# Low parts of streamed weights: a negation on ScalarE and an accumulating DMA in place of a subtraction on VectorE or GpSimd

## The chip, the cores and the metric

The kernel runs on one core of a Trainium2 chip. The metric is the device time of one execution in microseconds (us), the median of several runs.

## What is computed

A bidirectional encoder trunk on 16 meta tokens and 512 real tokens, 1024 features, float32. Four layers stand one after the other: latent attention (MLA), differential attention, a bidirectional recurrent block (RG-LRU), and MLA again. Each is followed by a SwiGLU feed-forward block, and each of these eight sub-layers has an RMS norm before and after it.

```python
for i in range(DEPTH):
    u = _rms_norm(h, g[0])
    u = _mla(u, ...)            # i = 0, 3; _diff_attn for i = 1, _rglru_block for i = 2
    h = h + _rms_norm(u, g[1])
    u = _swiglu(_rms_norm(h, g[2]), ffn_w_in[i], ffn_w_out[i])
    h = h + _rms_norm(u, g[3])
return h[:, N_META:]
```

## The kernel before

Activations lie feature-major in SBUF, 128 features by 528 tokens, so that each projection takes its weights as the stationary operand. A float32 operand x is split into x = h + l: h is x rounded to float32r, l is the rest. A product is three passes, `xh wh`, `xl wh` and `xh wl`, that add up in PSUM (`mm3`, L340 to L346; the matmul is L327). For a block of 128 input features TensorE takes the three in that order, on two ranges of 272 and 256 tokens. So it needs a block's `wl` last, and a `wl` that isn't there stops it at the third pass, since it works in order.

The weights are packed on the host into 456 chunks in the order of their use: mostly 1024 columns (512 KB), else 768, 640 or 512. Class `Weights` streams them. `fetch` loads a chunk with a DMA on SyncE's queue into one of two buffers `ws`. `ensure` makes the parts: ScalarE casts `ws` to `wh` (L261), and the engine named in `l_engine` subtracts, `wl = ws - wh` (L262). There are four pairs of `wh` and `wl`. `next` hands a chunk out and first calls `ensure` for the chunk two later (`ahead=2`), and each `ensure` asks for the load of the chunk two later still.

The order of the work is the order in which the program is written: each engine has one in-order queue, and a manual schedule keeps the written order. So where the calls of `next` and `ensure` stand decides what is ahead of a cast on ScalarE and ahead of a subtraction on its engine.

`run` goes through eight stages, each a sub-layer; `boundary` ends one and starts the next. In a boundary the residual is updated in two halves of the tokens, and the first three output tiles of the next projection are made from four chunks. `l_engine` is GpSimd in the even stages (MLA, differential attention, RG-LRU) and in most of a boundary, and VectorE in the odd stages (feed-forward) and for the last two chunks that a boundary prepares:

```python
self.W.l_engine = nc.vector if s % 2 else nc.gpsimd
```

Further work of GpSimd: the sums of squares `acc` and `acc2` (L321), rotary products, gates and sums of the recurrent block. In MLA the output projection is worked off in groups of four heads: a chunk pair for it is prepared once a group is done (`wo`, three times between the heads of each MLA).

Names used: `ws` loaded chunk, `wh` and `wl` its parts, `xh` and `xl` the parts of the normed input, `ql` the low part of a query tile, `p` a tile of softmax values (scaled at L769), `pa` and `pb` tiles in PSUM, `hh` and `hl` the parts of the hidden tiles of the feed-forward block.

Of the kernel before, what the change touches and what calls it, by code (L numbers as in the profile page):

```python
"""Bidirectional hybrid encoder trunk (MLA, differential attention, RG-LRU, MLA, each with a
SwiGLU mixer) on one core.

Activations are held feature-major, [128 features, token], so that every projection takes its
weights as the stationary operand in the layout they come in.  A float32 operand x is split
exactly into x = h + l, h being x rounded to float32r and l the rest; a product is the three
float32r passes hh + hl + lh, accumulated in float32.
"""
# [42 lines left out]
def spans(t0):  # L51
    """The ranges of tokens that a product takes at a time: 512 columns fill a bank of PSUM."""
    return ((t0, NT),) if t0 else halves(0)


def col0(t0):
    """The column in PSUM of token 0 of an output tile that starts with token t0."""
    return 512 - t0 if t0 else 512 - SPLIT
# [5 lines left out]
# ---------------------------------------------------------------- weight stream layout  # L64
# [4 lines left out]
def weight_plan():  # L69
    """The weight chunks in the order the program consumes them: for each, its blocks as  # L70
    (array, index into it, first row, columns)."""
# [105 lines left out]
# columns of the table of small parameters  # L177
S_NORM = 0                      # layer, which, k
S_MLA = S_NORM + DEPTH * 4 * NK  # j, 5 (q 3, kv 2)
S_SUB = S_MLA + 10  # L180
S_CW = S_SUB + 1                # 4 taps x 12
S_CB = S_CW + 48                # 12
S_BG = S_CB + 12                # direction, gate, 12
S_LL = S_BG + 48                # direction, 12
S_N = S_LL + 24                 # then 4 * 64 for lambda, the same on every partition

# [15 lines left out]
def shape_tables():  # L202
    """Rotary cosines and signed sines in the layout [x1 x2 x1 x2] x token, -|q - k| as a band, and
    for the first 32 queries, repeated."""
# [11 lines left out]
def f32(ap):  # L216
    return ap.bitcast(F32)


class Shifted:  # L220
    """An SBUF tile that is indexed as the output tile in PSUM it was copied from."""
# [8 lines left out]
class Weights:  # L230
    """Streams the weight chunks: DMA in, split into the float32r parts."""
# [8 lines left out]

    def fetch(self, upto):
        while self.n_dma < min(upto + 1, len(self.widths)):
            j = self.n_dma
            n = self.widths[j]
            t = self.k.wpool.tile([P, 1024], F32, name="ws", tag="ws", bufs=2)
            self.k.nc.sync.dma_start(
                out=t[:, 0:n],
                in_=self.dram[self.offs[j]:self.offs[j] + P * n].rearrange("(p n) -> p n", p=P))
            self.stage[j] = t
            self.n_dma += 1  # L250

    def ensure(self, upto):
        upto = min(upto, self.low + self.BUFS - 1, len(self.widths) - 1)
        while self.n_split <= upto:
# [7 lines left out]
            self.l_engine.tensor_tensor(out=wl[:, 0:n], in0=s[:, 0:n], in1=f32(wh[:, 0:n]), op=ALU.subtract)  # L262
# [12 lines left out]
    def retire(self, n):  # L275
        """All products with the first n of the held chunks have been traced."""
        self.low += n


class Trunk:  # L280
# [26 lines left out]
    # ---------------------------------------------------------------- small helpers  # L307
# [32 lines left out]
    def mm3(self, outs, wh, wl, xh, xl, start, stop, louts=None):  # L340
        """outs[i] += (wh + wl)^T (xh[i] + xl[i]) without the l l term; louts are the outputs for the
        xl[i], if those come in other ranges."""
# [5 lines left out]
    def xr(self, k, rng, hrng=None):  # L348
        """The two halves of input tile k: h parts (or those of the ranges hrng) and l parts."""
        hs = [self.xh[:, k, a:b] for a, b in hrng or rng]  # L350
        ls = [self.xl[k, int(a >= SPLIT)][:, a - (SPLIT if a >= SPLIT else 0):b - (SPLIT if a >= SPLIT else 0)]
              for a, b in rng]
        return hs, ls
# [5 lines left out]
    def project(self, t0=0, mid=None, ahead=2):  # L359
        """One output tile of 128 features from the normed input, K = 1024; mid is traced halfway."""  # L360
# [12 lines left out]
    def project_parts(self, done):  # L373
        """The same in four parts to be traced apart; done gets the finished tile."""
# [15 lines left out]
    # ---------------------------------------------------------------- norms  # L390
    def rstd(self, ps, out, inv_n, late=False):
        """out = 1 / sqrt(ps * inv_n + eps): the table's value, then a Newton step (returned to be
        traced later, if late)."""
# [9 lines left out]
    def stat(self, srcs):  # L403
        """Sums over the partitions of the given [128, w] tiles, on every partition."""
# [6 lines left out]
    # ---------------------------------------------------------------- between sub-layers  # L411
# [13 lines left out]
    def evict_u(self, m, view, a, b, g, add):  # L425
        """Keep u * g of output tile m and add its squares."""
# [21 lines left out]
    def residual(self, k, a, b, g2, first, last):  # L448
        """h += (u g) r on a half of tile k, and the next sub-layer's input from it, in three
        steps that are traced apart."""  # L450
# [33 lines left out]
    def load_x(self, k, half):  # L484
        """Two tiles of the input on a half of the tokens."""
# [13 lines left out]
    def boundary(self, tail, g1, g2, t0, first=False, last=False, after=None):  # L499
        """Ends a sub-layer (tail traces its last output tiles, one half of the tokens after the  # L500
        other) and starts the next one: the residual update, the norm, and the first three output
        tiles of the next projection."""
# [6 lines left out]
        def adv(n):  # L509
            """Traces n more steps of the updates, three tiles in flight."""  # L510
# [105 lines left out]
    def lead(self, get_chunks, kt, n, nk, t0=0):  # L616
        """The products of the first n output tiles with the first nk blocks: for each tile, in parts
        of two blocks to be traced apart."""
# [15 lines left out]
    def final(self, get_chunks, kt, g1, t0, split, add=False):  # L634
        """Output projection: all but the last split tiles; returns the tail for those, which traces
        a tile on a range of tokens, with mid called part of the way through and done after each
        chunk of weights that isn't the last."""
# [48 lines left out]
    def paired(self, g):  # L686
        """get_chunks for group g of four blocks of an output projection whose chunks hold two tiles each."""
# [6 lines left out]
    def chunked(self, sizes):  # L694
        """get_chunks for an output projection whose tiles each take chunks of these sizes."""
# [10 lines left out]
    # ---------------------------------------------------------------- SwiGLU  # L706
# [32 lines left out]
    # ---------------------------------------------------------------- multi-head latent attention  # L739
    def rope(self, ps, scale, t0, eng):  # L740
        """cos * x + sin * swap(x) of a [x1 x2 x1 x2] tile, times scale."""
# [13 lines left out]
    def softmax_max(self, p, ps, rows):  # L755
        """Takes a [rows, 528] tile of scaled scores from PSUM, negated, with minus its maximum along
        the free axis."""
# [5 lines left out]
    def softmax_exp(self, p, st, rows):  # L763
        """exp(s - max s) and its sums."""
# [7 lines left out]
    def transpose_p(self, ptiles, qts, kt, c0=C0, fold=None):  # L772
        """Columns kt of the P [q, k] tiles as a tile of P^T [k, q] in PSUM (for tile 0 with the 16
        columns that follow); fold, if given, picks the rows of query tile 0 and adds them."""
# [11 lines left out]
    def put_pt(self, ps, kt, t0):  # L786
        """The float32r parts of a tile of P^T; for tile 0 stacked, h h l."""
# [11 lines left out]
    def meta_values(self, n, width):  # L799
        """n tiles [96, width] for the values of the first 16 keys, stacked h l h, with zeros between."""  # L800
# [9 lines left out]
    def put_meta(self, vm, src):  # L810
        """Fills the rows of such a tile from [16, width] in PSUM."""
# [9 lines left out]
    def pv(self, outs, pt, kt, vm, vh, vl, t0):  # L821
        """Adds key tile kt to O^T = V^T P^T, held as two half tiles."""
# [9 lines left out]
    def mla(self, tiles, i, j, t0):  # L832
# [149 lines left out]
        def attend(h):  # L982
            """Scores and softmax of head h, between the transposes and products with the values
            of head h - 1; yields what is left of the latter."""
# [118 lines left out]
    def ps_like_rope(self, t):  # L1103
        """Rotary embedding of the shared key, from SBUF."""
# [11 lines left out]
    # ---------------------------------------------------------------- differential attention  # L1116
    def diff(self, tiles, i):
# [11 lines left out]
        def place(d, x, h, dtype):  # L1129
            """A tile of head h in one of its two places, which hold first its norm, then its parts."""  # L1130
# [32 lines left out]
        def scaled_q(h, dst, ps):  # L1163
            """q / 8 / slope of head h, the slope being the power of two 2^-(h + 1)."""
# [15 lines left out]
        def put_v(h, ps):  # L1180
            """Values of head h, token-major."""
# [16 lines left out]
        def more():  # L1198
            """Traces the next fillings."""
# [7 lines left out]
        def attend(h):  # L1207
            """Scores and softmaxes of head h, between the transposes and products with the values
            of head h - 1 and what there is to fill in."""
# [4 lines left out]
            def trail(n):  # L1214
                """exp of tile n, the scaling of tile n - 1, the difference of tile n - 2."""
# [22 lines left out]
            def score_meta(st):  # L1238
                """Query tile 0: component 0 in rows 0:16, component 1 in rows 32:48."""
# [72 lines left out]
        def sub_norm(hs):  # L1312
            """Per-head RMS norms of O^T over its 128 features, from their squares."""
# [64 lines left out]
        def first_half(m):  # L1378
            """The products of output tile m with the first four heads, in two parts."""
# [40 lines left out]
    # ---------------------------------------------------------------- RG-LRU  # L1420
    def lru_consts(self):
        """8 softplus(-lambda) and its negative, [128, 24] each (direction, tile)."""
# [250 lines left out]
```

## Time and profile before

| | |
|---|---|
| runs | 3310.26, 3317.22, 3307.76 us; median 3310.26 |
| profiled execution | span 3308.6 us from its first to its last instruction; its time outside the span isn't listed apart from the runs |
| mean granted TensorE clock | 0.978 |
| TensorE matmul, weight load | 3128.2 us (95%), 2905.0 us (88%) |
| VectorE, ScalarE, GpSimd | 1880.8 us (57%), 1394.0 us (42%), 751.8 us (23%) |
| read from HBM | 225.34 MB, 69 GB/s over the span |

The profile is of one execution. Busy time of an engine is the union of its instructions. PE is TensorE's matmul, PEld its weight load, DVE is VectorE, ACT is ScalarE, POOL is GpSimd, SP is SyncE; a q behind a name is the engine's queue. An L with a number is a line of the kernel. In lines that group instructions the form is out<-in with buffer numbers left out.

### The profile page before, as it was taken

The numbers are of one execution on the slowest core, as the hardware profiler recorded it, in microseconds if no ns is written. First come the engines' busy times: TensorE is split into PE (matmuls) and PEld (weight loads), VectorE is DVE, ScalarE is ACT, GpSimd is POOL, SyncE is SP. The second block draws the span as 40 slices with busy tenths as digits, with TensorE's granted clock in tenths as the row PEclk, the third lists the DMA queues.
The fourth block names the chain that finished last, engine by engine and source line by source line (L and its number), as shares of the span: only waits on it lengthen the run. The fifth ranks groups of instructions, "written<-read, shape, count | busy, mean of one in ns | idle before, by whom it ended". The sixth has DMA issues, their size and how long they took to land. (4 is left out here: it accounts for less than half of the span.)

```text
span 3308.6 us, 53371 instructions
## 1 busy us (share of the span) xinstructions
PE 3128.2 (95%) x22368; PEld 2905.0 (88%) x22368; DVE 1880.8 (57%) x2993; ACT 1394.0 (42%) x2464; POOL 751.8 (23%) x514
## 2 busy tenths in 40 slices
PE   8999999999989998999988889999998999999998
PEld 7888888999978888999977889999987787788887
DVE  7766667443186767444278874544257666674433
ACT  5544445222255665222245554322235554452222
POOL 3223123000144534000045543000033322330001
PEclk9999999999999999999998999999999999999999
DMA  3111012222211111322321112222321111122232
GB/s 100 31 44 43 27 48 72 90 90 92 89 65 46 39 45 57 98 90 88 97 72 58 64 58 90 90 90 88 95 77 39 46 30 47 58 72 93 95 100 79
DMA packets 71600, 230.88 MB, mean 70 GB/s; under 512 B 7824, under 2 KB 12304, under 8 KB 71360
## 3 DMA queue, kind: packets, MB, share of 16 engines
q1 hardware_dynamic: 70144, 225.54, 21.5%
q8 instruction: 176, 2.88, 0.4%
q10 hardware_dynamic: 1216, 1.93, 0.2%
q14 instruction: 64, 0.52, 0.1%
HBM read 225.34 MB, written 2.10 MB: 69 GB/s over the span
## 5 line engine op out<-in xcount | busy, mean ns | idle before, releaser
L327 PE MATMUL pa<-xh,wh 128*128 128x272 f32 (+2 forms) x4120 | 956.6, 304 | 17.4 <-ACT xh L318 7.6
L327 PE MATMUL pa<-xh,wl 128*128 128x272 f32 (+2 forms) x3776 | 892.3, 299 | 3.5 <-POOL wl L262 3.5
L327 PE MATMUL pa<-xl,wh 128*128 128x272 f32 (+1 forms) x3776 | 808.2, 287 | 43.9 <-DVE xl L324 42.9
L327 PEld LDWEIGHTS pa<-xl,wh 128*128 128x128 f32 x3776 | 619.3, 190 | 91.6 <-DVE xl L324 59.8
L327 PEld LDWEIGHTS pa<-xh,wh 128*128 128x128 f32 x4120 | 663.9, 190 | 36.2 <-DVE ql L324 9.1
L327 PEld LDWEIGHTS pa<-xh,wl 128*128 128x128 f32 x3776 | 614.4, 190 | 8.7 <-POOL wl L262 4.0
L262 DVE TENSOR_TENSOR wl<-ws,wh 128x1024 fp32r<-128x1024 f32 (+1 forms) x280 | 330.5, 1183 | 509.8 <-ACT wh L261 509.8
L262 POOL TENSOR_TENSOR wl<-ws,wh 128x1024 fp32r<-128x1024 f32 (+3 forms) x176 | 387.7, 2208 | 763.7 <-ACT wh L261 619.8
L321 POOL TENSOR_TENSOR acc<-acc,t 128x256 f32<-128x256 f32 (+3 forms) x158 | 165.2, 1045 | 1528.3 <-ACT t L318 1524.1
L261 ACT CAST wh<-ws 128x1024 fp32r<-128x1024 f32 (+3 forms) x456 | 440.4, 980 | 156.8 <-DMA ws<-in_w 142.0
L321 DVE TENSOR_TENSOR t<-pa,r 128x528 f32<-128x528 f32 (+1 forms) x193 | 135.5, 703 | 282.1 <-PE pa L327 282.1
L327 PE MATMUL pa<-hh,wl 128*128 128x272 f32 (+2 forms) x1078 | 249.2, 301 | 0.0
L327 PE MATMUL pa<-hl,wh 128*128 128x272 f32 (+2 forms) x1078 | 247.9, 300 | 0.0
L327 PE MATMUL pa<-hh,wh 128*128 128x272 f32 (+2 forms) x1078 | 247.1, 299 | 0.0
L793 ACT CAST pth<-pa 128x528 fp32r<-128x528 f32 (+3 forms) x200 | 118.7, 593 | 269.7 <-PE pa L782 268.3
L337 ACT CAST hh<-t 128x528 fp32r<-128x528 f32 (+1 forms) x88 | 55.5, 630 | 400.9 <-DVE t L321 400.9
L318 ACT ACTIVATE t<-t 128x528 f32<-128x528 f32 (+3 forms) x121 | 72.2, 597 | 294.8 <-DVE t L321 294.2
L327 PEld LDWEIGHTS pa<-hh,wl 128*128 128x128 f32 x1078 | 171.1, 188 | 6.8
L327 PEld LDWEIGHTS pa<-hh,wh 128*128 128x128 f32 x1078 | 171.3, 189 | 5.9
L327 PEld LDWEIGHTS pa<-hl,wh 128*128 128x128 f32 x1078 | 169.4, 188 | 6.8
L321 DVE TENSOR_TENSOR ptl<-pa,pth 128x528 fp32r<-128x528 f32 (+1 forms) x160 | 111.8, 699 | 79.6 <-ACT pth L793 75.3
L782 PE MATMUL pa<-ident,p 128*128 128x128 f32 (+3 forms) x840 | 140.4, 282 | 2.7 <-DVE p L769 2.6
(285 smaller groups left out, 5244.2 us busy)
## 6 DMA issues: line engine op xcount, KB each, us to landing
ws<-in_w SPq DMA_DIRECT2D x344, 512.0 KB, 3.4
ws<-in_w SPq DMA_DIRECT2D x80, 384.0 KB, 3.4
ws<-in_w SPq DMA_DIRECT2D x16, 320.0 KB, 2.9
ws<-in_w SPq DMA_DIRECT2D x16, 256.0 KB, 2.7
out<-h SPq DMA_DIRECT2D x16, 128.0 KB, 1.7
h<-in_x SPq DMA_DIRECT2D x4, 272.0 KB, 3.7
h<-in_x SPq DMA_DIRECT2D x4, 256.0 KB, 4.0
cos<-in_tab ACTq DMA_DIRECT2D x2, 264.0 KB, 4.1
```

What stands on the lines that cost most here:

```text
L261: self.k.nc.scalar.copy(out=wh[:, 0:n], in_=s[:, 0:n])
L262: self.l_engine.tensor_tensor(out=wl[:, 0:n], in0=s[:, 0:n], in1=f32(wh[:, 0:n]), op=ALU.subtract)
L318: return self.nc.scalar.activation(out=out, in_=in_, func=func, **kw)
L321: return (eng or self.nc.vector).tensor_tensor(out=out, in0=a, in1=b, op=op)
L327: self.nc.tensor.matmul(out, lhsT=lhsT, rhs=rhs, start=start, stop=stop)
L337: self.nc.scalar.copy(out=oh, in_=src)
L782: self.nc.tensor.transpose(ps[0:kb - ka, c0 + qa:c0 + qb], ptiles[qt][0:qb - qa, ka:kb], self.ident[0:qb - qa, 0:qb - qa])
L793: self.nc.scalar.copy(out=hi[0:n, w], in_=src)
```

## The change

In `ensure` the subtraction goes. ScalarE writes -`wh` into the `wl` buffer (an activation, `Copy` with scale -1.0), and a DMA that GpSimd issues reads the chunk from HBM a second time and adds it there (`accum_op=ALU.add`), so that `wl` = -`wh` + chunk. The chunk's place in HBM is a method of its own now. `l_engine` is still set but no longer used. Comments are gone, and the lines below `fetch` stand three lower.

```diff
+    def chunk(self, j):
+        n = self.widths[j]
+        return self.dram[self.offs[j]:self.offs[j] + P * n].rearrange("(p n) -> p n", p=P)
+
     def fetch(self, upto):
...
-            self.k.nc.sync.dma_start(
-                out=t[:, 0:n],
-                in_=self.dram[self.offs[j]:self.offs[j] + P * n].rearrange("(p n) -> p n", p=P))
+            self.k.nc.sync.dma_start(out=t[:, 0:n], in_=self.chunk(j))
...
             self.k.nc.scalar.copy(out=wh[:, 0:n], in_=s[:, 0:n])
-            self.l_engine.tensor_tensor(out=wl[:, 0:n], in0=s[:, 0:n], in1=f32(wh[:, 0:n]), op=ALU.subtract)
+            self.k.act(wl[:, 0:n], f32(wh[:, 0:n]), AF.Copy, scale=-1.0)
+            self.k.nc.gpsimd.dma_start(out=wl[:, 0:n], in_=self.chunk(j), accum_op=ALU.add)
             self.parts[j] = (wh, wl)
```

Two places show what this does to the queues. The first is the entry of the first feed-forward stage on VectorE, before the change (`r` is the norm's factor, `t<-pa` the first work on the stage's tiles):

```order
L324 SCALAR_TENSOR_TENSOR r_75<-t_6132,r_75 128x272
L262 TENSOR_TENSOR wl_6137<-ws_5820,wh_6136 128x1024
L324 SCALAR_TENSOR_TENSOR t_6184<-pb_6180,r_75 128x256
L324 SCALAR_TENSOR_TENSOR t_6184<-t_6184,r_75 128x256
L324 SCALAR_TENSOR_TENSOR r_75<-t_6184,r_75 128x256
L262 TENSOR_TENSOR wl_6190<-ws_5882,wh_6189 128x1024
L321 TENSOR_TENSOR t_6199<-t_6178,r_75 128x528
L321 TENSOR_TENSOR t_6202<-pa_5912,r_75 128x528
```

and the same chunks after it, on GpSimd (L324 is now what L321 was, L265 is the accumulating DMA):

```order
L324 TENSOR_TENSOR acc2_73<-acc2_73,t_6160 128x256
L324 TENSOR_TENSOR acc2_73<-acc2_73,t_6169 128x256
L324 TENSOR_TENSOR acc2_73<-acc2_73,t_6176 128x256
L265 DMA wl_6188<-in_w 128x1024
L265 DMA wl_6242<-in_w 128x1024
L265 DMA wl_6266<-in_w 128x1024
```

The two low parts that stood on VectorE between the pieces of the norm are now DMAs on GpSimd's queue, behind the additions of squares of the boundary, of which the last three are shown.

The second place is ScalarE at the same entry, after the change (L263 is the cast, L321 an activation; `hh` is a part of a hidden tile):

```order
L263 CAST wh_6187<-ws_5870 128x1024
L321 ACTIVATE wl_6188<-wh_6187 128x1024
L610 COPY t_6230<-pa_5962 128x528
L321 ACTIVATE r_75<-pb_6232,eps_78 128x256
L321 ACT_TABLE_LOAD
L321 ACTIVATE junk_79<-eps_78 128x1
L263 CAST wh_6241<-ws_5933 128x1024
L321 ACTIVATE wl_6242<-wh_6241 128x1024
L321 ACTIVATE t_6252<-t_6252 128x528
L340 CAST hh0_6258<-t_6255 128x528
```

Behind each cast, and ahead of what followed it, stands the negation of the same chunk.

## Rows read from the trace of the kernel before

**Rows 1.** The page: busy time, share of the span and instructions of each engine.

```profile
PE 3128.2 (95%) x22368; PEld 2905.0 (88%) x22368; DVE 1880.8 (57%) x2993; ACT 1394.0 (42%) x2464; POOL 751.8 (23%) x514
```

**Rows 2.** Stretches: us; busy PE, PEld, DVE, ACT, POOL; granted clock, DMA share, GB/s.

```profile
30.00:502.00 472.00, 449.87 (x3284) 403.09 (x3283) 314.29 (x661) 228.27 (x469) 121.76 (x68) 0.96 0.14 42
549.00:904.00 355.00, 355.00 (x2910) 355.00 (x2909) 138.35 (x154) 100.45 (x134) 8.30 (x7) 1.00 0.29 92
947.00:1264.00 317.00, 299.45 (x2108) 268.01 (x2108) 212.87 (x440) 189.51 (x367) 135.47 (x102) 0.97 0.15 49
...
1709.00:1972.00 263.00, 216.40 (x1580) 211.20 (x1578) 219.30 (x196) 149.94 (x206) 137.08 (x67) 0.91 0.21 66
...
2477.00:2898.00 421.00, 396.50 (x2261) 329.46 (x2260) 281.10 (x555) 212.38 (x420) 119.92 (x68) 0.98 0.15 46
```

**Rows 3.** Waits: who waited for whom, us in total, times, longest us.

```profile
PE pa L327 <- DVE xl L324: 42.9, 55, 2.4
PE pa L327 <- DVE ql L324: 29.4, 16, 2.4
```

**Rows 4.** Timeline near 198 us: start us, us, engine, line, operation, form, idle before.

```profile
197.61 1.98 ACT L261 CAST wh<-ws 128x1024 fp32r<-128x1024 f32 x2
198.09 0.50 DVE L769 TENSOR_SCALAR p<-p,st 128x528 f32<-128x528 f32 x1
198.70 2.71 DVE L769 TENSOR_SCALAR p<-p,st 128x528 f32<-128x528 f32 x1
198.71 4.96 POOL L262 TENSOR_TENSOR wl<-ws,wh 128x1024 fp32r<-128x1024 f32 x2 [8.24 <-ACT wh L261]
201.44 2.79 DVE L321 TENSOR_TENSOR qsa<-t,qsa 64x528 fp32r<-64x528 f32 x1
202.02 0.40 PE L327 MATMUL pa<-xh,wl 128*128 128x272 f32 x2
```

**Rows 5.** Groups of L261 and L262 by shape: busy us, mean ns | idle before.

```profile
L261 ACT CAST wh<-ws 128x1024 fp32r<-128x1024 f32 x344 | 357.4, 1042 | 132.8 <-DMA ws<-in_w 125.1 <-PE pa L327 7.6
L261 ACT CAST wh<-ws 128x768 fp32r<-128x768 f32 x80 | 65.8, 835 | 12.0 <-PE pb L327 6.0 <-DMA ws<-in_w 4.9 <-PE pa L327 0.8
L262 DVE TENSOR_TENSOR wl<-ws,wh 128x1024 fp32r<-128x1024 f32 x236 | 289.1, 1225 | 262.0 <-ACT wh L261 262.0
L262 POOL TENSOR_TENSOR wl<-ws,wh 128x1024 fp32r<-128x1024 f32 x108 | 272.3, 2526 | 343.2 <-ACT wh L261 284.5 <-issue 46.1 <-DVE rpost L324 8.7
```

**Rows 6.** DMA: the loads' queue (packets, MB, share), and all 456 loads' time to landing.

```profile
q1 hardware_dynamic: 70144, 225.54, 21.5%
...
DMA to landing us min/median/max: 2.5/3.4/5.4
```

**Rows 7.** Timeline inside the first feed-forward stage.

```profile
579.86 1.05 ACT L261 CAST wh<-ws 128x1024 fp32r<-128x1024 f32 x1
589.85 0.41 PE L327 MATMUL pa<-xh,wl 128*128 128x272 f32 x2
595.72 0.41 PE L327 MATMUL pa<-xh,wl 128*128 128x272 f32 x2
```

**Rows 8.** Timeline at the entry of the first feed-forward stage.

```profile
545.62 1.04 ACT L261 CAST wh<-ws 128x1024 fp32r<-128x1024 f32 x1
548.80 0.41 PE L327 MATMUL pa<-xh,wl 128*128 128x272 f32 x2
```

**Rows 9.** Timeline at the end of the first feed-forward stage.

```profile
903.67 3.65 POOL L262 TENSOR_TENSOR wl<-ws,wh 128x768 fp32r<-128x768 f32 x2
907.51 0.29 PE L327 MATMUL pb<-hh,wl 128*128 128x272 f32 x1
```

**Rows 10.** Recurrent stage: two lines of the timeline, and the stretch behind them.

```profile
1961.25 2.82 POOL L262 TENSOR_TENSOR wl<-ws,wh 128x1024 fp32r<-128x1024 f32 x1
1964.12 0.51 PE L327 MATMUL pa<-xh,wl 128*128 128x272 f32 x2 [2.87 <-POOL wl L262]
...
1965.40:1968.80 3.40, 3.40 (x18) 3.40 (x17) 3.40 (x6) 3.17 (x6) 0.00 (x0) 0.50 0.27 104
```

## The prediction

> **What bounds the kernel now.** I read the page's busy times first: TensorE is busy for 95% of the span [rows 1]. So a faster VectorE is worth only what TensorE now idles, and a late operand costs in full. The table by stage says where it idles [rows 2]: in the feed-forward stage of 549 to 904 us TensorE is busy for 355.00 of 355.00 us, in the first latent attention (MLA) for 449.87 of 472, in the differential attention for 299.45 of 317, in the recurrent stage for only 216.40 of 263. The granted clock is 1.00 in the first and 0.96, 0.97 and 0.91 in the others. There is nothing to win in the four feed-forward stages, and 111 us of idle time in the four others (the second MLA has 24.5).
>
> The waits of TensorE say who ends it: `ql` and `xl` of VectorE above all [rows 3]. The timeline around 198 us says why [rows 4]: a softmax scaling that takes 0.50 us takes 2.71 us when GpSimd's subtraction starts beside it, and the next product, which reads two tiles, is as slow. So the removed work on GpSimd holds VectorE up, and TensorE waits for the end of that.
>
> **What is removed.** 280 subtractions on VectorE (236 of them 1225 ns) and 176 on GpSimd (108 of 2526 ns) [rows 5]. In the feed-forward stages that is work under a full TensorE: worth nothing. In the others I credit: of the 29.4 us for `ql` 70%, 21 us (most of those waits follow a pair of GpSimd subtractions); of the 42.9 us for `xl` 20%, 9 us, since much of it comes in the second half of a boundary, where GpSimd only adds squares; of the recurrent stage's idle 46.6 us 55%, 26 us (VectorE is busy for 219 of its 263 us, so what is taken off VectorE there counts); of the differential stage's 17.6 us 40%, 7 us. Idle time there also lowers the clock: 0.04 of 472, 0.09 of 263 and 0.03 of 317 us are 52 us of lost clock [rows 2]; I credit 40%, 21 us. Together **84 us**. None of it is credited in full, as GpSimd still issues 456 DMAs, and what those do to VectorE no row shows. Bounds: nothing, and some 140 us.
>
> **What is added.** ScalarE negates every chunk: its nearest row is the cast of the same tile, 1042 ns [rows 5], so 456 of these are about 440 us of an engine that is busy for 42%. They stand right behind the casts. I put their delay of other ScalarE work at 5 us, since the boundary's `xh` come behind them.
>
> What decides is the path from a cast to the product with `wl`. It was a cast and a subtraction; now it is a cast, a negation, and a DMA that starts only after the negation. No row shows an accumulating DMA or one issued by GpSimd. The nearest is the load of the same chunk from SyncE: median 3.4 us from issue to landing, 2.5 to 5.4; its packets take 21.5% of the span for 225.54 MB, so 1.65 us of all sixteen queues for 0.52 MB [rows 6]. An accumulation must read its destination too: I add one more pass, 1.65 us. The Trainium skill ("Collectives: The Full Stack", section "The bandwidth ceiling") says the same of adds inside a DMA: it blames their half rate on two source reads, not on the add; by it the second pass is also 1.65 us, and no run here shows it yet. GpSimd's issue I put, as an estimate, at 1.2 us, halfway between nothing and its pass over such a chunk [rows 5]. So the DMA takes 3.4 + 1.65 + 1.2 = 6.25 us, and with the negation **7.3 us** from the cast's end to a usable `wl` (6.7 us for 768 columns). Lower bound: 1.04 + 3.4 = 4.4 us. Upper: 1.04 + 2 x 5.4, near 12 us.
>
> Against this stands each chunk's margin, from the cast's end to the first product with `wl`:
> - Steady feed-forward: cast ends at 580.91, product at 589.85, margin 8.94 us, the next chunk 5.87 us later [rows 7]. It holds. The queues hold too: 1.65 + 3.3 = 4.95 us for each 5.87.
> - Stage entries: the cast ends at 546.66, the product starts at 548.80: margin 2.1 us [rows 8]. Four feed-forward entries and three others are like this: 7 x 5.2 = 36 us. GpSimd's queue has the last of twelve additions ahead of that DMA there, but it is done by the negation's end.
> - Attention output chunks: cast over by 198.71, product at 202.02, margin 3.4 [rows 4]; three in each MLA: 6 x 3.9 = 23 us.
> - Ends of the feed-forward stages (768 columns): cast over by 903.67, product at 907.51, margin 3.8 [rows 9]: 4 x 2.9 = 12 us.
> - Recurrent stage, where GpSimd's order and not the cast starts the low part: 1961.25, product 1964.12 [rows 10]; 6.25 - 2.9 = 3.4, twice: 7 us.
> - Eight more (start, first MLA chunks, output of the recurrent stage) at 3.3, a little under the others' mean: 27 us.
>
> That is 105 us at 27 places. The chunks behind a feed-forward entry have small margins as well, but their casts hang on VectorE's and ScalarE's chain, from which 1.2 us subtractions go: 2 us each, 8 us. And a stall costs clock: after the 2.87 us at 1964 the granted clock is 0.50 (1.2 GHz) for 3.4 us [rows 10], so 1.7 us lost; I take that for half of 27 places, 23 us. ScalarE's 5 us included, the loss is **141 us**.
>
> **Sum.** 141 - 84 = +57 us on the profiled span of 3308.6; the runs' median stands 1.7 us above that span. So 3367 us.
>
> **Rivals.**
> 1. *The low part is too late everywhere.* From 8.9 us on, each pair of chunks in a feed-forward stage waits as well. At 10 us it is 1.06 us for each of some 84 pairs, 89 us, and 27 x 2.7 = 73 us more at the tight places: 3530 us, and the queues would be close to full (if an accumulation takes over 4.2 us of all sixteen, they bound the stage). For it: loads and accumulations start at about the same moment, since the load's buffer is now free at the cast's end, and the longest landing is 5.4 us [rows 6]. Against it: the loads use 29% of the queues there [rows 2]. Chance 0.2.
> 2. *The relief wins; faster.* One us of latency is worth about 27 us. Below 5.2 us the sum turns. With a DMA as quick as a plain load (latency 4.4 us) the places cost 33 us, clock and ScalarE 10, and the relief is 84: 3270 us. For it: [rows 4], where the two subtractions visibly cost VectorE over 4 us, and 111 us of idle time. Against it: the second read and GpSimd's issue. Chance 0.2.
> 3. *GpSimd's issue holds VectorE up as its subtraction did.* Then only a third of the relief comes: 57 us more, but 6 less at the attention chunks, where a later TensorE hides it: 3420 us. For it: the exclusion in [rows 4]; against it: an issue is shorter than 2.5 us. The Trainium skill ("SBUF — State Buffer", section "Who interferes with whom") has a rule against this change: VectorE in its two-port modes and GpSimd lock each other out, and a GpSimd-issued DMA waits for its descriptors. The 2.71 us scaling agrees as to the lock; of descriptors no row here tells. Chance 0.2.
>
> That the change does not do what it says is excluded by the instruction order: no subtraction is left, and 456 negations and 456 DMAs stand there.
>
> **Numbers.** Forecast 0.4, rivals 0.2 each. The forecast's own spread is some 40 us either way (a latency of 6 to 8.5 us, relief of 60 to 110). A measurement here tells 0.3%, 10 us, from no change. Faster: rival 2 and a little of the forecast, 0.21. Same: 0.08. Slower: 0.71. The range of 3285 to 3545 takes in most of rivals 1 and 2 and all of 3.
>
> **What would show it.** Right: TensorE's waits for `wl` move to DMAs, 3 to 5 us each at entries and attention output chunks; `ql` waits shrink, the scaling takes 0.5 us again; feed-forward interiors keep 355 of 355; DMA share there rises from 0.29 to some 0.8; the accumulating DMA lands in about 6 us. Wrong: landings over 8 us with waits inside the feed-forward stages (rival 1), landings under 4.5 us (rival 2), or slow VectorE pieces beside each issue (rival 3).

## The result and the profile after

The changed kernel takes 3393.9 us (median of 4 runs, 3389.5 to 3396.0), the kernel before on the same chip 3313.7 us. The ratio is 1.0242, with a 95% interval of 1.0220 to 1.0264: slower by 2.4%. The profiled execution has a span of 3387.8 us, 79.2 us more than before. First the page: busy times and two groups (lines that stood below 262 are now three higher, so that L330 is the matmul and L321 the activation), the DMA queues (packets, MB, share), and four of the DMA issues (count, KB each, us to landing).

```profile
PE 3153.4 (93%) x22368; PEld 2927.6 (86%) x22368; DVE 1401.5 (41%) x2713; ACT 1838.3 (54%) x2920; POOL 750.6 (22%) x794
...
L265 POOL DMA_DIRECT2D wl<-in_w x456 | 395.2, 868 | 2054.4 <-ACT wl L321 1836.8
...
L321 ACT ACTIVATE wl<-wh 128x1024 fp32r<-128x1024 f32 (+3 forms) x456 | 454.3, 996 | 14.5
```

```profile
q0 software_dynamic: 65664, 221.28, 38.8%
q1 hardware_dynamic: 70144, 225.54, 20.2%
...
ws<-in_w SPq DMA_DIRECT2D x344, 512.0 KB, 3.5
wl<-in_w POOLq DMA_DIRECT2D x344, 512.0 KB, 6.3
...
ws<-in_w SPq DMA_DIRECT2D x16, 256.0 KB, 2.7
wl<-in_w POOLq DMA_DIRECT2D x16, 256.0 KB, 4.8
```

Beside [rows 1], VectorE has lost 479 us of work and ScalarE has got 444. TensorE, the bound, is busy for 25.2 us more with the same 22368 matmuls, and its idle time went from 180.4 to 234.4 us: 54.0 us. The two make up the 79.2. The accumulating DMA lands in 6.3 us, counted from the start of its issue (as all landings here are), and its queue takes almost twice the time of the plain loads' queue for about the same bytes (221.28 and 225.54 MB). Who ends TensorE's idle time now, against [rows 3]:

```profile
PE pa L330 <- DMA wl<-in_w: 110.7, 38, 6.8
PE pa L330 <- DVE xl L327: 28.7, 48, 1.7
PE pb L330 <- DMA wl<-in_w: 21.8, 5, 6.0
PE pa L330 <- ACT pth L796: 13.8, 8, 1.8
...
PE pa L330 <- DVE ql L327: 4.2, 2, 2.1
```

The old waits have shrunk (`ql` from 29.4 to 4.2 us, `xl` from 42.9 to 28.7). In their place stand 43 waits for the new DMA, 132.5 us, and one that was not there, for ScalarE's `pth` (the rounded part of the transposed softmax values, which ScalarE casts out of PSUM). The same stages as in [rows 2], moved to where they now lie:

```profile
43.00:520.00 477.00, 446.69 (x3281) 401.88 (x3280) 274.22 (x651) 262.03 (x506) 71.78 (x68) 0.96 0.35 77
573.00:929.00 356.00, 355.18 (x2906) 354.97 (x2905) 59.41 (x85) 160.80 (x191) 61.58 (x68) 1.00 0.80 179
982.00:1306.00 324.00, 309.35 (x2156) 277.56 (x2157) 197.12 (x433) 220.66 (x402) 95.97 (x106) 0.96 0.41 93
1764.00:1982.00 218.00, 202.30 (x1578) 199.61 (x1577) 166.96 (x188) 178.59 (x236) 78.12 (x68) 0.97 0.69 152
```

The feed-forward stage is all but untouched (355.18 us busy of 356.00), though the DMA share went from 0.29 to 0.80. The recurrent stage does its 1578 matmuls in 218 us (263 before). So there is a large gain in one place and a larger loss elsewhere. One place of the loss is the entry of the first feed-forward stage, in the timeline (start us, us, engine, line):

```profile
563.46 1.03 ACT L263 CAST wh<-ws 128x1024 fp32r<-128x1024 f32 x1
...
564.53 1.06 ACT L321 ACTIVATE wl<-wh 128x1024 fp32r<-128x1024 f32 x1
...
565.89 0.88 POOL L265 DMA_DIRECT2D wl<-in_w  x1 [1.60 <-PE pb L330]
...
571.39 0.81 PE L330 MATMUL pa<-xh,wl 128*128 128x272 f32 x2 [4.50 <-DMA wl<-in_w]
```

The cast ends at 564.49. In [rows 8] the product came 2.1 us after that, here it comes 6.9 us after: 1.1 for the negation, 0.3 until GpSimd issues, 5.5 for the DMA. TensorE stands still for 4.50 us. The windows of that stall and of what follows it:

```profile
566.80:571.40 4.60, 0.10 (x2) 0.02 (x1) 3.07 (x6) 4.04 (x6) 0.73 (x1) 0.93 0.91 185
571.40:575.00 3.60, 3.60 (x19) 3.60 (x20) 1.57 (x3) 1.93 (x3) 0.13 (x1) 0.61 0.92 203
575.00:580.00 5.00, 5.00 (x43) 5.00 (x43) 1.42 (x2) 1.50 (x3) 0.87 (x1) 1.00 0.65 162
```

After the stall the granted clock is 0.61 on average over 3.6 us, so partly at its lower level (1.2 GHz): 1.4 us more, which stand in the busy column, not in the idle time. TensorE does 19 matmuls there in 3.6 us, and 43 in the next 5.0.

At the first attention output chunk, [rows 4] before, the stall is longer:

```profile
203.14 1.06 ACT L321 ACTIVATE wl<-wh 128x1024 fp32r<-128x1024 f32 x1
204.50 0.87 POOL L265 DMA_DIRECT2D wl<-in_w  x1 [9.54 <-ACT wl L321]
...
206.52 0.87 POOL L265 DMA_DIRECT2D wl<-in_w  x1 [1.15 <-ACT wl L321]
...
212.31 0.81 PE L330 MATMUL pa<-xh,wl 128*128 128x272 f32 x2 [5.66 <-DMA wl<-in_w]
```

From issue to product are 7.8 us here, against 5.5 at the entry: two chunks are prepared together, and while TensorE waits (206.65 to 212.30) the DMA share is 0.97.

### The profile page after: what moved, and what is told of

The parts are those of the page before. It is cut to its first block, busy times and chain, and to the rows that moved or that the text cites. A ratio compares the mean times of both kernels' runs of the same rounds, so it can differ in the third digit from the quotient of the medians.

```text
span 3387.8 us, 54134 instructions
## 1 busy us (share of the span) xinstructions
PE 3153.4 (93%) x22368; PEld 2927.6 (86%) x22368; DVE 1401.5 (41%) x2713; ACT 1838.3 (54%) x2920; POOL 750.6 (22%) x794
## 3 DMA queue, kind: packets, MB, share of 16 engines
q0 software_dynamic: 65664, 221.28, 38.8%
q1 hardware_dynamic: 70144, 225.54, 20.2%
## 5 line engine op out<-in xcount | busy, mean ns | idle before, releaser
L330 PE MATMUL pa<-xh,wl 128*128 128x272 f32 (+2 forms) x3776 | 908.7, 304 | 90.9 <-DMA wl<-in_w 90.9
L330 PE MATMUL pa<-xh,wh 128*128 128x272 f32 (+2 forms) x4120 | 970.4, 308 | 12.4 <-ACT xh L321 9.8
L265 POOL DMA_DIRECT2D wl<-in_w x456 | 395.2, 868 | 2054.4 <-ACT wl L321 1836.8
L330 PE MATMUL pa<-xl,wh 128*128 128x272 f32 (+1 forms) x3776 | 813.3, 289 | 29.5 <-DVE xl L327 28.7
L330 PEld LDWEIGHTS pa<-xh,wl 128*128 128x128 f32 x3776 | 625.1, 193 | 102.7 <-DMA wl<-in_w 97.3
L330 PEld LDWEIGHTS pa<-xh,wh 128*128 128x128 f32 x4120 | 677.9, 193 | 31.6 <-ACT xh L321 10.9
L330 PEld LDWEIGHTS pa<-xl,wh 128*128 128x128 f32 x3776 | 625.6, 191 | 75.6 <-DVE xl L327 43.1
L263 ACT CAST wh<-ws 128x1024 fp32r<-128x1024 f32 (+3 forms) x456 | 445.2, 976 | 76.5 <-PE pa L330 48.1
L321 ACT ACTIVATE wl<-wh 128x1024 fp32r<-128x1024 f32 (+3 forms) x456 | 454.3, 996 | 14.5
L324 DVE TENSOR_TENSOR t<-pa,r 128x528 f32<-128x528 f32 (+1 forms) x193 | 135.5, 703 | 667.5 <-PE pa L330 667.5
L330 PE MATMUL pa<-hh,wl 128*128 128x272 f32 (+2 forms) x1078 | 249.5, 301 | 5.4 <-DMA wl<-in_w 5.4
L330 PE MATMUL pa<-hl,wh 128*128 128x272 f32 (+2 forms) x1078 | 248.1, 300 | 0.0
L324 DVE TENSOR_TENSOR acc<-acc,t 128x272 f32<-128x272 f32 (+2 forms) x18 | 8.3, 463 | 578.5 <-ACT t L321 574.9
L330 PE MATMUL pa<-hh,wh 128*128 128x272 f32 (+2 forms) x1078 | 247.1, 299 | 0.0
L324 POOL TENSOR_TENSOR acc<-acc,t 128x256 f32<-128x256 f32 (+3 forms) x158 | 164.9, 1044 | 324.1 <-ACT t L321 321.4
L321 ACT ACTIVATE t<-t 128x528 f32<-128x528 f32 (+3 forms) x121 | 72.0, 595 | 205.6 <-DVE t L324 205.6
L330 PEld LDWEIGHTS pa<-hh,wl 128*128 128x128 f32 x1078 | 171.1, 189 | 13.4 <-DMA wl<-in_w 6.9
L330 PEld LDWEIGHTS pa<-hh,wh 128*128 128x128 f32 x1078 | 171.2, 189 | 6.0
L330 PEld LDWEIGHTS pa<-hl,wh 128*128 128x128 f32 x1078 | 169.3, 188 | 6.7
L321 ACT ACTIVATE t<-pa 128x528 f32<-128x528 f32 (+2 forms) x46 | 27.7, 602 | 252.3 <-PE pa L330 252.3
```

Source lines behind the costliest of these rows:

```text
L263: self.k.nc.scalar.copy(out=wh[:, 0:n], in_=s[:, 0:n])
L265: self.k.nc.gpsimd.dma_start(out=wl[:, 0:n], in_=self.chunk(j), accum_op=ALU.add)
L321: return self.nc.scalar.activation(out=out, in_=in_, func=func, **kw)
L324: return (eng or self.nc.vector).tensor_tensor(out=out, in0=a, in1=b, op=op)
L330: self.nc.tensor.matmul(out, lhsT=lhsT, rhs=rhs, start=start, stop=stop)
```

## The experiments

My theory: two separate things happen. Taking the subtractions away gains some 80 us, mostly in the even stages; the longer path from a cast to a usable low part costs more, at places where TensorE's margin is shorter than that path, and nothing elsewhere. The rivals: ScalarE's load costs the time, GpSimd's issues hold VectorE up as its subtractions did, or the relief is small.

**The addition left out.**

```diff
             self.k.act(wl[:, 0:n], f32(wh[:, 0:n]), AF.Copy, scale=-1.0)
-            self.k.nc.gpsimd.dma_start(out=wl[:, 0:n], in_=self.chunk(j), accum_op=ALU.add)
```

> The accumulating DMA is left out, so the low parts hold only the negated high parts and the added chunk is missing from the output; the negation on ScalarE stays. Theory (the change gains by taking the subtractions away and loses by low parts that land late): the 132.5 us of TensorE's waits for the DMAs into wl vanish, and the clock that they cost; by the prediction's terms 3308.6 - 84 + 5, so 3230 us, and between 3215 and 3250. Rival (ScalarE's 456 negations cost far more than 5 us, the waits for pth and xh with them): over 3275 us, with these waits still there. Rival (the relief is small): 3300 us or more with no wait for wl.

Measured: 3220.3 us, ratio 0.9726 (0.9696 to 0.9757); span 3214.6. Its page and the first of TensorE's waits:

```profile
PE 3102.0 (96%) x22368; PEld 2882.0 (90%) x22368; DVE 1382.9 (43%) x2713; ACT 1835.5 (57%) x2920; POOL 357.6 (11%) x338
```

```profile
PE pa L329 <- DVE xl L326: 28.7, 43, 1.7
PE pa L329 <- ACT pth L795: 13.8, 8, 1.8
PE pa L329 <- ACT xh L320: 10.1, 5, 5.9
```

This separates the two halves of the change. Relief with ScalarE's cost: 3308.6 - 3214.6 = 94.0 us. What the DMA costs: 3387.8 - 3214.6 = 173.2 us, of which 51.4 are busy time of TensorE (3153.4 - 3102.0; the mean clock is 0.987 here and 0.969 with the DMA) and 121.8 idle time (132.5 of waits for `wl`, less 10.7 of other waits that these stalls hide). ScalarE's load is not the loss: it is all here. It does cost something, the 13.8 us for `pth`. And the issues hold VectorE little: with 456 of them it is busy for 18.6 us more, 41 ns for each, and 7.5 of these us lie in a few taps of the recurrent stage (see the last section).

**A plain DMA in the place of the accumulating one.**

```diff
-            self.k.nc.gpsimd.dma_start(out=wl[:, 0:n], in_=self.chunk(j), accum_op=ALU.add)
+            self.k.nc.gpsimd.dma_start(out=wl[:, 0:n], in_=self.chunk(j))
```

> GpSimd issues a plain DMA into wl in place of the accumulating one, so the low parts hold the chunk itself and the subtraction of the high part is left out of the output; order, issue, HBM traffic and the wait for the negation stay. Theory (the accumulation's own second pass takes 1.65 us of the 6.3 us): landing about 4.7 us, the 43 stalls shorter by 1.6 us each and some clock back, 3300 to 3325 us, queue share of these DMAs near 20%. Rival (the landing time is the issue by GpSimd and the two transfers side by side): landing stays near 6.3 us, 3390 us. If the landing were that of SyncE's loads, 3.5 us, about 3265 us.

Measured: 3332.3 us, ratio 1.0051 (1.0034 to 1.0068). Its queue, issues, landing and the two waits for `wl`:

```profile
q0 software_dynamic: 65664, 221.28, 22.6%
...
L265 POOL DMA_DIRECT2D wl<-in_w x456 | 246.2, 540 | 2137.4 <-ACT wl L321 1943.7
...
wl<-in_w POOLq DMA_DIRECT2D x344, 512.0 KB, 4.7
```

```profile
PE pa L330 <- DMA wl<-in_w: 71.2, 25, 5.5
...
PE pb L330 <- DMA wl<-in_w: 14.1, 5, 4.0
```

The landing is what the theory says, 1.6 us shorter. The time is 7 us above my range: 61 us gained against the changed kernel, since the shorter transfer leaves 85.3 us of the 132.5. The accumulation costs 0.388 x 3387.8 / (0.226 x 3336.2) = 1.74 times the queues' time of a plain DMA, and 0.33 us more of GpSimd for each issue (868 against 540 ns). So one us of latency is worth 61 / 1.6, some 38 us; I had said 27. (One expectation below writes 37.) The two profiled executions, which differ by 51.6 us, would make it 32.

**All subtractions on VectorE**, in the kernel before.

```diff
-            self.l_engine.tensor_tensor(out=wl[:, 0:n], in0=s[:, 0:n], in1=f32(wh[:, 0:n]), op=ALU.subtract)
+            self.k.nc.vector.tensor_tensor(out=wl[:, 0:n], in0=s[:, 0:n], in1=f32(wh[:, 0:n]), op=ALU.subtract)
```

> The kernel before, with all 456 subtractions on VectorE: no DMA, no negation, and GpSimd has no subtraction. Theory A (what holds VectorE up is GpSimd's subtraction beside it): the scaling of p takes 0.5 us throughout, the waits for ql of 29.4 us fall to under 8, the recurrent stage's 263 us shorten by 20 or more; 3255 to 3290 us although VectorE gets 176 subtractions of 1.2 us more. Theory B (it is the amount of VectorE's own work that counts): VectorE, busy for 219 of 263 us there, becomes the bound of the recurrent stage; 3310 us or slower.

Measured: 3266.5 us, ratio 0.9846 (0.9829 to 0.9863). The scaling, whose longest was 2.71 us before, and the recurrent stretch between the first products with `wl` of chunks 223 and 255 (261.00 us before):

```profile
L769 DVE TENSOR_SCALAR p<-p,st x144: 481/496/889, 74.3 to 2831.7; 128x528 f32<-128x528 f32 x128, 16x528 f32<-16x528 f32 x16
```

```profile
1705.90:1936.80 230.90, 202.79 (x1538) 198.47 (x1536) 205.42 (x223) 148.37 (x205) 63.58 (x36) 0.94 0.22 72
```

Theory A holds, with `ql` waits of 7.9 us: VectorE gets 176 subtractions more, and is busy for only 17.3 us more in the whole kernel (1898.1 against 1880.8), while in the recurrent stretch it is busy for 13 us less (205.42, before 218.39). The removed work on GpSimd had been lengthening VectorE's own instructions. No DMA is needed for this half of the relief (3308.6 - 3263.9 = 44.7 of the 94.0 us).

**By place**: VectorE subtracts, except inside the even stages.

```diff
+    ADDED = {*range(5, 48), *range(121, 150), *range(223, 255), *range(345, 388)} - {18, 28, 38, 358, 368, 378}
...
-            self.k.act(wl[:, 0:n], f32(wh[:, 0:n]), AF.Copy, scale=-1.0)
-            self.k.nc.gpsimd.dma_start(out=wl[:, 0:n], in_=self.chunk(j), accum_op=ALU.add)
+            if j in self.ADDED:
+                self.k.act(wl[:, 0:n], f32(wh[:, 0:n]), AF.Copy, scale=-1.0)
+                self.k.nc.gpsimd.dma_start(out=wl[:, 0:n], in_=self.chunk(j), accum_op=ALU.add)
+            else:
+                self.k.nc.vector.tensor_tensor(out=wl[:, 0:n], in0=s[:, 0:n], in1=f32(wh[:, 0:n]), op=ALU.subtract)
```

> The negation and the accumulating DMA only inside the even stages, without the first attention-output chunk of each group (chunks 5 to 47, 121 to 149, 223 to 254 and 345 to 387 but for six); everywhere else VectorE subtracts. Theory (gain and loss lie at different places): almost all waits for wl go, the relief in the even stages stays; 3225 to 3265 us, faster than before by 1.5% or more. Rival (the relief needs VectorE free at the boundaries and in the feed-forward stages too, or DMAs in the even stages slow others): 3290 us or more. If theory A of the run with all subtractions on VectorE holds and VectorE's work costs nothing, the two runs come out alike within 10 us.

Measured: 3278.7 us, ratio 0.9885 (0.9867 to 0.9904). Faster than before, but outside my range, and 12 us behind the run with VectorE everywhere. Its waits say why:

```profile
PE pa L334 <- DMA wl<-in_w: 29.4, 18, 5.7
PE pa L334 <- ACT pth L800: 13.8, 8, 1.8
```

In the recurrent stretch it gains (214.1 us against 230.9), in both MLAs it loses (556.4 against 539.8 up to chunk 52, 518.0 against 508.7 from 338 to 392): there the subtraction on VectorE cost less than what now takes its place. The wait for `pth` (none in the run with VectorE everywhere) comes with the negations, the first chunks of the two MLAs wait for their DMAs (3.54 and 3.97 us), and one more place, chunk 223 ahead of the recurrent stretch, waits for 5.70 us.

**Halves.**

```diff
-            self.k.act(wl[:, 0:n], f32(wh[:, 0:n]), AF.Copy, scale=-1.0)
-            self.k.nc.gpsimd.dma_start(out=wl[:, 0:n], in_=self.chunk(j), accum_op=ALU.add)
+            for a, b in ((0, n // 2), (n // 2, n)):
+                self.k.act(wl[:, a:b], f32(wh[:, a:b]), AF.Copy, scale=-1.0)
+                self.k.nc.gpsimd.dma_start(out=wl[:, a:b], in_=self.chunk(j)[:, a:b], accum_op=ALU.add)
```

> The changed kernel with each negation and each accumulating DMA in two halves of the columns, so the first half can start after half a negation and is a smaller transfer (256 KB, 4.8 us in the changed kernel). The first half is usable about 2 us sooner (0.5 of negation, 1.5 of transfer). Theory (the loss is latency against margin at some 43 places): by the plain-DMA run, where 1.65 us less were worth 61 us, about 74 us less than the changed kernel's 3394, so 3310 to 3330 us, with the waits for wl near 60 us. Rival (912 issues on GpSimd and the fixed part of a DMA eat it): second halves come late, waits for wl stay above 110 us, 3380 us or more.

Measured: 3353.5 us, ratio 1.0109 (1.0086 to 1.0132). A gain of about 40 us where I expected 64 to 84; the time lies between my range and the rival's. The issues and the landing:

```profile
L266 POOL DMA_DIRECT2D wl<-in_w x912 | 811.3, 1064 | 1675.3 <-ACT wl L322 1519.6
...
wl<-in_w POOLq DMA_DIRECT2D x688, 256.0 KB, 6.3
```

A half lands in 6.3 us, not in 4.8: the first of the two in 5.9, the second in 6.7 (medians). An issue's record is 1.06 us long on average, but the two of a chunk overlap: GpSimd is busy for 811.3 us with 912 of them, 0.89 each. So only the half negation and part of the transfer are won; the waits for `wl` fall to 88.9 us. That the halves are late because they share the queues with each other is my reading. A half also moves in pieces of half the length, and no run separates the two.

**The negation first.**

```diff
-            self.k.nc.scalar.copy(out=wh[:, 0:n], in_=s[:, 0:n])
-            self.k.act(wl[:, 0:n], f32(wh[:, 0:n]), AF.Copy, scale=-1.0)
+            self.k.act(wl[:, 0:n], s[:, 0:n], AF.Copy, scale=-1.0)
+            self.k.nc.scalar.copy(out=wh[:, 0:n], in_=s[:, 0:n])
```

> The changed kernel with ScalarE's two instructions of a chunk exchanged: the negation is made from the loaded chunk and stands ahead of the cast, so that the DMA starts one cast (1.04 us) sooner and the high part comes one negation later. Same instructions, same DMAs. Theory: waits for wl shorter by about 1 us at each of 43 places, 37 us less by the plain-DMA run's 37 us for each us of latency: 3345 to 3365 us. Rival (the high part then comes too late at the same places, or what counts is ScalarE's load and not the order): 3385 us or more, with new waits for wh.

Measured: 3349.2 us, ratio 1.0104 (1.0084 to 1.0124), 45 us below the changed kernel; the waits for `wl` are 96.9 us, 35.6 less. The same instructions in another order give back more than half of the loss. Both landings became longer (3.5 and 6.3 us in the changed kernel). That fits with where the next load now starts: 0.7 us after the accumulation's issue, where it started 1.4 us ahead of it (medians).

```profile
ws<-in_w SPq DMA_DIRECT2D x344, 512.0 KB, 6.3
wl<-in_w POOLq DMA_DIRECT2D x344, 512.0 KB, 6.9
```

**VectorE inside all stages**, GpSimd still in the boundaries and at the ends of stages.

```diff
-            self.W.l_engine = nc.vector if s % 2 else nc.gpsimd
+            self.W.l_engine = nc.vector
```

> The kernel before, where only the line in the loop over the stages sets l_engine to VectorE throughout; GpSimd keeps its subtractions in the boundaries and at the ends of stages. Theory (GpSimd's subtraction costs by holding VectorE up inside the even stages; at a boundary VectorE is itself the chain, so a subtraction is better off on GpSimd there): faster than all on VectorE by what the stretch around the first MLA's end lost there (7.6 us of 99.4) and the second's (4.9), so 3245 to 3262 us. Rival (holding VectorE up costs as much in the boundaries): 3268 us or more.

Measured: 3254.1 us, ratio 0.9806 (0.9792 to 0.9821). One line of the kernel before gives 1.9%. The stretch of chunks 38 to 48, the end of the first MLA, takes 96.9 us here and 107.0 with VectorE everywhere: in a boundary GpSimd's subtraction is the better one. That VectorE is itself the chain there is the theory that forecast it; no run shows the chain by itself.

**Mixed**: the same, with the accumulating DMA for 22 chunks inside the recurrent stage (the edit in `ensure` as in the run by place, with `l_engine` in the second branch).

```diff
+    ADDED = {*range(225, 254)} - {233, 235, 240, 244, 245, 249, 250}
...
-            self.W.l_engine = nc.vector if s % 2 else nc.gpsimd
+            self.W.l_engine = nc.vector
```

> As the run with VectorE inside all stages, but 22 chunks inside the recurrent stage (225 to 253 without 233, 235, 240, 244, 245, 249 and 250) by negation and accumulating DMA. Theory (the accumulating DMA pays only where VectorE is the bound and the margin is over 8 us): the recurrent stretch, 261 us before and 230.9 with all on VectorE, takes 212 to 220 us, so 11 to 18 us less than that run: 3230 to 3248 us, faster than both kernels by over 2%. Rival (VectorE is not the bound there once GpSimd's subtraction is gone): no gain over that run.

Measured: 3237.8 us, ratio 0.9764 (0.9747 to 0.9781), the fastest kernel of the study that does the whole computation: 4.7% below the changed kernel (0.9764 / 1.0242). The recurrent stretch without and with these DMAs:

```profile
1691.70:1925.20 233.50, 200.61 (x1539) 195.35 (x1537) 204.65 (x223) 148.04 (x205) 62.02 (x36) 0.96 0.21 71
```

```profile
1690.80:1912.00 221.20, 198.24 (x1539) 194.77 (x1537) 178.00 (x201) 169.51 (x227) 71.49 (x58) 0.96 0.53 127
```

12.3 us less there; that stretch itself came out 1.2 us over my range of 212 to 220, and 9.7 us below the 230.9 from which I had reckoned 11 to 18.

The stages side by side, in us, each from one chunk's first product with `wl` to another's (from the timelines; the first row from the start of the span):

| stretch (chunks) | before | changed | no addition | VectorE everywhere | VectorE in stages | mixed |
|---|---|---|---|---|---|---|
| first MLA (to 52) | 554.7 | 578.6 | 543.5 | 539.8 | 536.3 | 534.7 |
| feed-forward, inside (52 to 114) | 349.8 | 350.9 | 349.8 | 349.8 | 349.8 | 349.8 |
| differential (114 to 154) | 411.7 | 429.2 | 408.0 | 416.9 | 407.3 | 407.8 |
| recurrent (223 to 255) | 261.0 | 216.6 | 204.0 | 230.9 | 233.5 | 221.2 |
| its output (255 to 276) | 108.6 | 131.6 | 106.5 | 109.2 | 109.8 | 109.8 |
| second MLA (338 to 392) | 515.2 | 551.8 | 497.0 | 508.7 | 507.6 | 503.4 |

## Why the prediction came out as it did

The forecast was slower, 3367 us; 3394 us is inside the range of 3285 to 3545 and 27 us above the forecast. The mechanism was the right one: relief in the even stages, latency against margin elsewhere. Point by point:

- **Latency.** I put the DMA at 6.25 us and it lands in 6.3, but of other parts, so that the total is luck. GpSimd's issue is 0.87 us where I took 1.2. The second pass is about 1.3 us and not 1.65: the accumulating DMA lands 1.6 us after the plain one (6.3 - 4.7), but 0.33 of these are its longer issue; and by the queues' time (38.8% of 3387.8 us and 22.6% of 3336.2 us, each for 221.28 MB) 512 KB take 3.1 us of all sixteen queues, and 1.8 with the plain DMA. What fills the gap is a part that I had not named: even a plain DMA from GpSimd takes 1.3 us longer to land than SyncE's load (4.7 against 3.4 us in the same run). The Trainium skill ("Collectives: The Full Stack", section "The bandwidth ceiling") blames two source reads for the halved rate of an add in a collective; the queue's time of 1.74 plain transfers agrees in direction and is a little under two.
- **Feed-forward interiors** hold, as forecast: 350.9 us for 349.8. The queues hold too; the DMA share of 0.80 is the one I named.
- **The late places** were under-sized by 19 us. Their sum from the timeline is 132.2 us at 41 places (the two others of the 43 waits are under 0.2 us each):

| places | forecast, us | measured, us |
|---|---|---|
| 7 stage entries | 36 | 31.8 |
| 6 attention output chunks | 23 | 33.6 |
| 4 ends of feed-forward stages | 12 | 15.7 |
| inside the recurrent stage | 7 (2 places) | 11.2 (7 places) |
| start, output of the recurrent stage | 27 (8) | 31.8 (10) |
| chunks in and behind feed-forward stages | 8 | 8.0 (7) |

 At the entries I was a little high; at the attention output chunks I was low by 10.6, because I gave each DMA the same 6.25 us, where these take 7.4 to 7.8 from issue to product. Two chunks are prepared together there, so I put it down to the queues that they share.
- **The clock after stalls** is the term that failed most: 23 us forecast, for half of the places; 51.4 us measured as TensorE's busy time that comes with the stalls. At the entry, the clock lost 1.4 us after one stall (I had 1.7 from [rows 10]), but other stalls cost more. In the trace's record of the clock 25 of the 43 waits have a stretch at the lower level at their end or behind it, at 2.1 us of lost clock each; I had taken 13.5 places at 1.7. So both the number of places and the cost of each were too small.
- **ScalarE.** 5 us forecast. The new wait for `pth` is 13.8 us, with or without the DMA, and is absent where no negations run. The first MLA, where the run without the addition is 7.2 us slower than VectorE in stages (543.5 against 536.3), points the same way.
- **Relief.** 84 - 5 = 79 us forecast, 94.0 measured. The 94.0 are the run without the addition. In the changed kernel the `ql` waits gave 25.2 of 29.4 us (I credited 21), the `xl` waits 14.2 (9). The recurrent stage gave most: 57.0 us between its chunks 223 and 255 without the addition (44.4 in the changed kernel). TensorE's idle time fell from 49.5 to 11.8 us there, 76%, where I credited 55%. The differential stretch gave only 3.7 us where I credited 7, and TensorE's busy time fell by 26.2 us (3128.2 - 3102.0) where I credited 21 for the clock.
- **The sum.** Loss 173.2, relief 94.0, net +79.2; forecast 141 - 5 = 136, 79 and +57. Both sides were under-sized and the errors partly cancel.
- **The rivals.** *Too late everywhere*: not so; inside the feed-forward stages TensorE waits at a handful of chunks, 2.0 us at most. *The relief wins*: its condition was a latency under 5.2 us. By the plain DMA's 32 to 38 us per us, the changed kernel's +80 us would be gone with 2.1 to 2.5 us less, from 7.7 us (1.06 + 0.3 + 6.3) to between 5.2 and 5.6; the plain DMA, at 6.1, was still 0.5% slower than before. The range was said to take in most of this rival, but the rival's own 3270 us lie below it. *GpSimd's issue holds VectorE up*: the scaling never takes more than 0.904 us in the changed kernel, and only two taps of the recurrent stage were held for long.

```profile
L772 DVE TENSOR_SCALAR p<-p,st x144: 482/496/904, 86.7 to 2944.1; 128x528 f32<-128x528 f32 x128, 16x528 f32<-16x528 f32 x16
```

The Trainium skill ("SBUF — State Buffer", section "Who interferes with whom") has VectorE in its two-port modes and GpSimd lock each other out, and DMAs issued by GpSimd wait for their descriptors. The lock agrees with what went away here (2.71 us to 0.90); a long wait for descriptors does not show: the 456 issues take between 851 and 1165 ns.

What I did not see is that most of the relief needed no DMA. Of the 94 us, 56.9 come from one line that keeps the subtraction but gives it to VectorE (span 3251.7); what was read from [rows 4] was a property of GpSimd's subtraction, not of subtractions. In the recurrent stage the DMA did add to it: 12.3 us of the mixed run.

## What to carry to other kernels

When work is moved from an engine to a DMA, compare the new path's latency with the margin at each place where the consumer is tight, not with the average: here half the chunks (the feed-forward interiors, margin 8.9 us) hid 7.7 us at next to no cost, and 41 others paid 132 us of stall and 51 us of clock. Before that, ask which part of the old work hurts: if it is contention between two engines, moving the same instruction to the one that was held up can give more than removing it. And charge a stall of TensorE with the slow clock behind it, here about 0.4 us for each us of stall.

## What the runs showed of the hardware that I had not expected

- An accumulating DMA costs GpSimd more to issue than a plain one of the same shape: 868 against 540 ns. A plain DMA from GpSimd takes 1.3 us longer to land than the load of as many bytes from SyncE (4.7 against 3.4 us, both in the plain-DMA run). Two DMAs for the halves of a chunk land about as late as the whole did (5.9 and 6.7 us against 6.3).
- The convolution taps of the recurrent stage were the hidden part of the relief. The group of L324 on VectorE by shape (busy us, mean ns | idle before), in the kernel before:

```profile
L324 DVE SCALAR_TENSOR_TENSOR xc<-t,sm,xc 128x527 f32<-128x527 f32 x24 | 42.2, 1758 | 0.7
```

 and in the run with VectorE inside all stages:

```profile
L324 DVE SCALAR_TENSOR_TENSOR xc<-t,sm,xc 128x527 f32<-128x527 f32 x24 | 24.4, 1019 | 0.7
```

 The same 24 instructions take 1758 ns beside GpSimd's subtractions and 1019 ns without them.
- A DMA's issue with GpSimd's products behind it can still hold VectorE for long. In the changed kernel two such taps take 5977 and 6361 ns; in the run without the addition the longest takes 1742 ns. All 36 taps of the changed kernel, and the timeline of VectorE and of GpSimd at the first of the two:

```profile
L327 DVE SCALAR_TENSOR_TENSOR xc<-t,sm,xc x36: 752/769/6361, 1761.7 to 1919.7; 128x527 f32<-128x527 f32 x24, 128x526 f32<-128x526 f32 x12
```

```profile
1813.23 8.54 DVE L327 SCALAR_TENSOR_TENSOR xc<-t,sm,xc 128x526 f32<-128x526 f32 x3
```

```profile
1814.33 0.86 POOL L265 DMA_DIRECT2D wl<-in_w  x1
1814.93 5.46 POOL L324 TENSOR_TENSOR g<-g,xc 128x528 f32<-128x528 f32 x4
```

 Three taps take 8.54 us (2.38 undisturbed) while GpSimd, released by its DMA's issue, runs four products in a row; the middle tap lasts from just after the first product's start until they are over. The run without the addition has the same three taps and the same four products, with no issue ahead of them:

```profile
1742.20 5.24 DVE L326 SCALAR_TENSOR_TENSOR xc<-t,sm,xc 128x526 f32<-128x526 f32 x3
```

```profile
1743.32 6.80 POOL L323 TENSOR_TENSOR g<-g,xc 128x528 f32<-128x528 f32 x4
```

 There each tap takes 1.72 to 1.73 us. So four products in a row do not hold a tap for 6 us by themselves. Each of the six kernels with GpSimd's DMAs in this stage has a tap of 5.7 to 6.9 us right behind an issue, the plain DMA too (5697 ns), and the three without them and without GpSimd's subtractions there have none over 2 us. Whether the issue itself does it, or the moment at which it lets the products start, is not shown.
